# Output projection of a hybrid decoder layer: two blocks of rows by seven products of half depth instead of eight

## The chip, the cores and the metric

The kernel runs on one core of a Trainium2 chip. Its time is the device time of one execution in microseconds (us); three runs are given by their median. The engines are called as the profile calls them: PE (TensorE; PEld its weight loads), DVE (VectorE), ACT (ScalarE), POOL (GpSimd) and SP (SyncE, which issues the DMA transfers).

## The reference

One layer on a sequence of 4096 rows of 1024 columns, in float32. Attention (8 heads, three dilated windows) gives 512 columns, an HGRN2 recurrence (4 heads) the other 512; both are normed per head, gated, and set side by side. The change concerns the last lines:

```python
y_attn = _head_rmsnorm(attn, attn_out_norm_w[layer], ATTN_HEADS) * jax.nn.silu(ag.astype(f32))
y_hgrn = _head_rmsnorm(rec, hgrn_out_norm_w[layer], HGRN_HEADS) * jax.nn.silu(hg.astype(f32))
mixed = jnp.concatenate([y_attn, y_hgrn], axis=-1).astype(x.dtype)
x = x + mixed @ w_out[layer]          # (4096 x 1024) @ (1024 x 1024)
...
return _rmsnorm(x, final_norm_w)
```

## The kernel before

The work stands in three stages: the input projection of attention (the start to about 720 us), then the projections of HGRN interleaved with the attention heads, then the end of attention and the output projection (from about 2370 us).

Every float32 operand is split into a high part and a low part (the rest), and a product is made of three matmuls that add into one PSUM bank: high by high, high by low, low by high. A split is one copy on ACT (the high part) and one subtraction (the low part) on DVE or POOL. The stationary operand of a matmul here is a 128x128 piece of rows transposed, the moving one 128x512 of a weight.

`two` opens four PSUM pools: four banks `att`, two `proj`, one `po`, one `hp1`. A scheduler orders each engine's instructions by its own estimate of when they can run; all DMA transfers are issued by SP, one after the other, in an order that is fixed when the kernel is built. An instruction whose operand is not ready holds up all that stand behind it on its engine.

The mixed rows pass through a tensor in memory, `y_d`. The attention's last step, `finish` (L588 to L630), takes eight blocks of rows of a head: PE transposes (L614, L615) into an `att` bank, DVE multiplies them by weights into the tile `pr` (L617, four times), POOL adds (L620, L621), DVE makes the inverse norm `nrr` in small steps (L625, L626, then L133 to L141), POOL multiplies (L628, L629), and a DMA stores to `y_d` (L630). There is one `pr` tile: the next finish's L617 waits until that store is done.

The output projection goes over 32 blocks of 128 rows. `load_y` reads a block of `y_d` in two halves, transposes them on PE (eight transposes, L885) and splits them (L170, L171). `project` (L183 to L185) makes 24 matmuls of 128x512 for each half of the columns. `residual` adds x on DVE (L915), `final_norm` squares on ACT (L922), scales on DVE (L925) and stores. The weights of the first half of the columns lie in `whi` and `wlo`; those of the second half are split (L873, L874) into `w1hi` and `w1lo`, which take over the tiles `QS` and `KH` once the attention's scores (L434, L435) are done with them; `xr4`, four blocks of x, takes over `KL`.

The input projection already has the form that the change brings to the output projection: `summed_w` builds sums and differences of weight quarters, `load_unit` those of the rows, and `half` (L730 to L736) makes one product of half depth, 12 matmuls.

Of the kernel before, what the change touches and what calls it, by code (L numbers as in the profile page):

```python
# [27 lines left out]
S = 4096  # L28
D = 1024
NB = 32  # L30
KT = 8
# [18 lines left out]
def layer(ctx: ExitStack, tc: tile.TileContext, x, xT, xP, pos, w_in, w_out, nw, anw, hnw, lbraw, fnw,  # L50
          ident_in, mask_in, trih_in, invf_in, out):
    nc = tc.nc
    V, A, G, T = nc.vector, nc.scalar, nc.gpsimd, nc.tensor
    dma = nc.sync.dma_start
# [7 lines left out]
    y_d = dram.tile([S, D], F32, name="y_d")  # L62
# [4 lines left out]
    ident = const.tile([128, 128], F32, name="ident")  # L67
# [5 lines left out]
    wp = mid.enter_context(tc.tile_pool(name="wp", bufs=8))  # L73
    xp = mid.enter_context(tc.tile_pool(name="xp", bufs=2))
# [91 lines left out]
    def split_tile(src, lo_eng, pool, tag, bufs):  # L166

        t = pool.tile([128, 1024], F32R, name=tag, bufs=bufs)
        hi, lo = t[:, 0:512], t[:, 512:1024]
        A.activation(hi, src, AF.Copy)  # L170
        lo_eng.tensor_tensor(lo, src, hi.bitcast(F32), op=ALU.subtract)  # L171
        return t

    def parts(t):
        return t[:, 0:512], t[:, 512:1024]

    def project(X, W):
        ps = ps_t.tile([128, 512], F32, name="att")
        for k in range(KT):
            hi, lo = X[k // 4]  # L180
            c = slice((k % 4) * 128, (k % 4 + 1) * 128)
            whi, wlo = W[k]
            T.matmul(ps, hi[:, c], whi, start=(k == 0), stop=False)  # L183
            T.matmul(ps, hi[:, c], wlo, start=False, stop=False)  # L184
            T.matmul(ps, lo[:, c], whi, start=False, stop=(k == KT - 1))  # L185
        return ps

    def load_pair(t, g):

# [470 lines left out]
    def plain_w(P, j):  # L660

        res = []
        for k in range(4):
            raw = fetch_w(2 * P, 4 * j + k, xp, "raw", 3)
            hi = wp.tile([128, 512], F32R, name="whi", bufs=8)
            lo = wp.tile([128, 512], F32R, name="wlo", bufs=8)
            s = nwt[:, 4 * j + k : 4 * j + k + 1]
            A.activation(hi, raw, AF.Copy, scale=s)
            V.scalar_tensor_tensor(lo, raw, s, hi.bitcast(F32), op0=ALU.mult, op1=ALU.subtract)
            res.append((hi, lo))  # L670
        return res
# [58 lines left out]
    def half(ps, X, W, start=True):  # L730
        for k in range(4):
            c = slice(k * 128, (k + 1) * 128)
            (hi, lo), (whi, wlo) = X, W[k]
            T.matmul(ps, hi[:, c], whi, start=start and k == 0, stop=False, skip_group_check=not start)  # L734
            T.matmul(ps, hi[:, c], wlo, start=False, stop=False, skip_group_check=not start)  # L735
            T.matmul(ps, lo[:, c], whi, start=False, stop=(k == 3), skip_group_check=not start)  # L736

    def plain_products(t, X, W, C0, third=True):

        pa = ps_m.tile([128, 512], F32, name="m")  # L740
        half(pa, X["A11"], W["B11"])
        u2 = p1p.tile([128, 512], F32, name="u2", bufs=2)
        A.activation(u2, pa, AF.Copy)
        pe = None
        if third:
            pe = ps_m.tile([128, 512], F32, name="m")
            half(pe, X["S4"], W["B22"])
        half(pa, X["A12"], W["B21"], start=False)
        A.activation(C0[:, 0], pa, AF.Copy, scale=rstd[:, 2 * t : 2 * t + 1])
        return u2, pe  # L750
# [30 lines left out]
    W = {"B11": plain_w(0, 0)}  # L781
# [5 lines left out]
    X = load_unit(0, tables_done)  # L787
# [3 lines left out]
    for P in range(2):  # L791
        if P:
            W = {"B11": plain_w(1, 0), "B21": plain_w(1, 1)}
# [34 lines left out]
    ps_p = ctx.enter_context(tc.tile_pool(name="ps_p", bufs=2, space=PSUM))  # L828
    ps_t = ctx.enter_context(tc.tile_pool(name="ps_t", bufs=4, space=PSUM))
    ps_o = ctx.enter_context(tc.tile_pool(name="ps_o", bufs=1, space=PSUM))  # L830
    ps_h = ctx.enter_context(tc.tile_pool(name="ps_h", bufs=1, space=PSUM))
    two = ExitStack()
    big = two.enter_context(tc.tile_pool(name="big", bufs=1))
    tp = two.enter_context(tc.tile_pool(name="tp", bufs=2))
    QS = big.tile([128, S], F32R, name="QS")
    KH = big.tile([128, S], F32R, name="KH")
    KL = big.tile([128, S], F32R, name="KL")
    OA = big.tile([128, S], F32, name="OA")
# [5 lines left out]
    att = hp.tile([128, 256], F32, name="att", bufs=1)  # L844
# [4 lines left out]
    X = load_pair(0, 4)  # L849
    W = list(load_w(4))  # L850
    for _ in range(4):
        next(queue[0])
    for g in range(4, 8):
        hvec = load_vec(hp, g - 4)
        for t in range(NB // 2):
            qd, kd, ea = hgrn_gates(t, project_T(X, W))
            hgrn_values(t, project_N(X, W))
            if (g, t) != (7, NB // 2 - 1):
                X = load_pair((t + 1) % (NB // 2), g + (t + 1) // (NB // 2))
# [3 lines left out]
        if g < 7:  # L863
            W = list(load_w(g + 1))


    def fetch_wo(n, k, rp, tag, bufs):
        raw = rp.tile([128, 512], F32, name=tag, bufs=bufs)
        dma(raw, w_out[k * 128 : (k + 1) * 128, n * 512 : (n + 1) * 512])
        return raw  # L870

    def split_wo(raw, hi, lo):
        A.activation(hi, raw, AF.Copy)  # L873
        V.tensor_sub(lo, raw, hi.bitcast(F32))  # L874
        return hi, lo

    def load_y(b):
        res = []
        for hf in range(2):
            yt = xp.tile([128, 512], F32, name="raw", bufs=3)  # L880
            dma(yt, y_d[b * 128 : (b + 1) * 128, hf * 512 : (hf + 1) * 512])
            pt_ = ps_p.tile([128, 512], F32, name="proj")
            for k in range(4):
                c = slice(k * 128, (k + 1) * 128)
                T.transpose(pt_[:, c], yt[:, c], ident)  # L885
            res.append(parts(split_tile(pt_, V, xp, "xs", 5)))
        return res

    WO = [[], []]
    for k in range(KT):  # L890
        raw = fetch_wo(0, k, xp, "raw", 3)
        WO[0].append(split_wo(raw, wp.tile([128, 512], F32R, name="whi", bufs=8), wp.tile([128, 512], F32R, name="wlo", bufs=8)))
    three.close()
    fp = two.enter_context(tc.tile_pool(name="fp", bufs=2))
    raws = [fetch_wo(1, k, fp, "woraw", 4) for k in range(4)]
    fnwt = fp.tile([128, D], F32, name="fnwt", bufs=1)
    dma(fnwt, fnw.partition_broadcast(128))
    take(10 ** 9)
    Y = [load_y(0), load_y(1)]
    ps0 = [project(Y[0], WO[0]), project(Y[1], WO[0])]  # L900
    w1hi = big.tile([128, S], F32R, name="w1hi", tag="QS")
    w1lo = big.tile([128, S], F32R, name="w1lo", tag="KH")
    xr4 = big.tile([128, S], F32, name="xr4", tag="KL")
    for k in range(KT):
        raw = raws[k] if k < 4 else fetch_wo(1, k, fp, "woraw", 4)
        c = slice(k * 512, (k + 1) * 512)
        WO[1].append(split_wo(raw, w1hi[:, c], w1lo[:, c]))
    xrs = {}

    def residual(b, n, ps):  # L910
        if b not in xrs:
            xrs[b] = xr4[:, b % 4 * D : (b % 4 + 1) * D]
            dma(xrs[b], x[b * 128 : (b + 1) * 128, :])
        cn = slice(n * 512, (n + 1) * 512)
        V.tensor_add(xrs[b][:, cn], ps, xrs[b][:, cn])  # L915

    def final_norm(b):
        xr = xrs.pop(b)
        ss = fp.tile([128, 2], F32, name="fss")
        for n in range(2):  # L920
            sq = fp.tile([128, 512], F32, name="fsq")
            A.activation(sq, xr[:, n * 512 : (n + 1) * 512], AF.Square, accum_out=ss[:, n : n + 1])  # L922
        V.tensor_add(ss[:, 0:1], ss[:, 0:1], ss[:, 1:2])
        r = rsqrt(fp, ss[:, 0:1], 1, 1.0 / D, EPS, "fr")
        V.scalar_tensor_tensor(xr, xr, r, fnwt, op0=ALU.mult, op1=ALU.mult)  # L925
        dma(out[b * 128 : (b + 1) * 128, :].rearrange("(u r) c -> r u c", r=16), xr)

    for b in range(2):
        residual(b, 0, ps0[b])
    for b in range(2):  # L930
        residual(b, 1, project(Y[b], WO[1]))
        final_norm(b)
    Yn = load_y(2)
    for b in range(2, NB):
        Yb, Yn = Yn, load_y(b + 1) if b + 1 < NB else None
        for n in range(2):
            residual(b, n, project(Yb, WO[n]))
        final_norm(b)
    two.close()
    mid.close()  # L940

# [47 lines left out]
```

## Time and profile before

| what | value |
|---|---|
| median of three runs | 2758.32 us (2758.07 to 2759.17) |
| the profiled execution | 2760.87 us, its span 2759.1 us |
| mean granted PE clock | 0.966 of full speed |
| busy: PE, DVE, ACT, POOL | 94%, 70%, 61%, 33% of the span |
| memory traffic | 346 MB read, 126 MB written |

The span runs from the first to the last recorded instruction or transfer. A busy share is a mean over stages. In rows of groups the columns are the line, the engine, the operation with output and inputs, their shapes, the count, then busy us and mean ns of one, and after the second bar the idle time of the engine just before them with what ended it. In rows of single instructions: start, duration, engine, line, and in brackets the idle time before it with its releaser. In a table by stretches, each engine's busy us with its count of instructions, then the granted clock, the share of the DMA engines and GB/s.

### The profile page before, as it was taken

The numbers are of one execution on the slowest core, as the hardware profiler recorded it, in microseconds if no ns is written. First come the engines' busy times: TensorE is split into PE (matmuls) and PEld (weight loads), VectorE is DVE, ScalarE is ACT, GpSimd is POOL, SyncE is SP. The second block draws the span as 40 slices with busy tenths as digits, with TensorE's granted clock in tenths as the row PEclk, the third lists the DMA queues.
The fourth block names the chain that finished last, engine by engine and source line by source line (L and its number), as shares of the span: only waits on it lengthen the run. The fifth ranks groups of instructions, "written<-read, shape, count | busy, mean of one in ns | idle before, by whom it ended". The sixth has DMA issues, their size and how long they took to land.

```text
span 2759.1 us, 51828 instructions
## 1 busy us (share of the span) xinstructions
PE 2596.6 (94%) x17330; PEld 2347.1 (85%) x17330; DVE 1936.2 (70%) x5202; ACT 1689.5 (61%) x4719; POOL 919.1 (33%) x900
## 2 busy tenths in 40 slices
PE   6899989999979999899999899999999997899998
PEld 4678867888869989899999899999999996688887
DVE  8777788777637788787787786776777777533443
ACT  8755565555548778678678686687686687222222
POOL 5456636656434464141241231331321421100000
PEclk8999999999979999899999999999999998899999
DMA  6864464444685776774864755746846644444442
GB/s 231 255 181 145 145 200 126 146 144 143 211 235 171 237 232 188 201 187 142 219 178 146 226 162 154 211 143 198 219 137 190 190 141 118 124 137 131 137 132 87
DMA packets 452190, 475.89 MB, mean 172 GB/s; under 512 B 119336, under 2 KB 334420, under 8 KB 451924
## 3 DMA queue, kind: packets, MB, share of 16 engines
q1 hardware_dynamic: 451924, 472.58, 58.0%
q8 instruction: 138, 2.26, 0.4%
q14 instruction: 128, 1.05, 0.1%
HBM read 346.06 MB, written 126.37 MB: 171 GB/s over the span
## 4 chain that ended last, share of the span: by engine, by line
PE 72%; DMA 10%; DVE 8%; ACT 4%; issue 2%; SPq 2%; POOL 2%; DVEq 0%; POOLq 0%; ACTq 0%
PE proj L210 19%; PE po L469 6%; PE m L736 5%; PE m L735 5%; PE m L734 5%; PE att L457 5%; PE att L183 4%; PE att L184 4%; PE att L185 4%; PE att L434 3%; PE att L435 3%; DMA raw<-xP 1%; DMA y_d<-pr 1%; PE proj L885 1%; DMA QS<-qk_d 1%
## 5 line engine op out<-in xcount | busy, mean ns | idle before, releaser
L210 PE MATMUL proj<-xs,whi 128*128 128x256 f32 x2048 | 431.6, 295 | 18.8 <-ACT whi L161 9.3
L210 PE MATMUL proj<-whi,xs 128*128 128x256 f32 x2048 | 432.5, 294 | 4.4 <-DVE hz L317 4.4
L210 PEld LDWEIGHTS proj<-xs,whi 128*128 128x128 f32 x2048 | 333.8, 194 | 25.0 <-ACT whi L161 10.7
L210 PEld LDWEIGHTS proj<-whi,xs 128*128 128x128 f32 x2048 | 335.8, 194 | 6.0 <-DVE hz L317 4.7
L445 DVE CUSTOM_DVE_ANT_0 pt<-att,mask 128x256 f32<-128x256 f32 (+1 forms) x768 | 269.4, 388 | 77.5 <-PE att L435 75.4
L210 PE MATMUL proj<-xs,wlo 128*128 128x256 f32 x1024 | 301.7, 295 | 0.6 <-DVE wlo L162 0.6
L210 PE MATMUL proj<-wlo,xs 128*128 128x256 f32 x1024 | 300.0, 293 | 0.0
L461 DVE TENSOR_TENSOR pl<-att,ph 128x512 fp32r<-128x512 f32 (+1 forms) x384 | 237.4, 625 | 57.5 <-ACT ph L460 53.3
L447 ACT ACTIVATE pt<-pt,ml 128x256 f32<-128x256 f32 (+1 forms) x512 | 238.1, 467 | 57.2 <-DVE ml L445 56.2
L457 PE MATMUL att<-ident,pt 128*128 128x128 f32 x1368 | 229.4, 281 | 5.7 <-ACT pt L447 3.9
L460 ACT ACTIVATE ph<-att 128x512 fp32r<-128x512 f32 (+1 forms) x384 | 203.0, 542 | 47.9 <-PE po L469 29.2
L469 PE MATMUL po<-ph,vh 128*128 128x128 f32 (+1 forms) x856 | 213.7, 279 | 7.2 <-issue 2.7
L469 PE MATMUL po<-pl,vh 128*128 128x128 f32 (+1 forms) x856 | 208.3, 289 | 2.9 <-DVE pl L461 2.9
L210 PEld LDWEIGHTS proj<-xs,wlo 128*128 128x128 f32 x1024 | 198.6, 194 | 2.3 <-issue 1.2
L210 PEld LDWEIGHTS proj<-wlo,xs 128*128 128x128 f32 x1024 | 198.0, 193 | 1.2 <-issue 1.0
L915 DVE TENSOR_TENSOR xr<-att,xr 128x512 f32<-128x512 f32 x64 | 44.3, 692 | 195.7 <-PE att L185 195.7
L469 PEld LDWEIGHTS po<-ph,vh 128*128 128x128 f32 x856 | 167.8, 196 | 12.1 <-issue 6.7
L457 PEld LDWEIGHTS att<-ident,pt 128*128 128x128 f32 x1368 | 163.1, 144 | 11.2 <-ACT pt L447 5.7
L469 PEld LDWEIGHTS po<-pl,vh 128*128 128x128 f32 x856 | 168.3, 197 | 4.2 <-DVE pl L461 3.7
L734 PE MATMUL m<-tw,ss 128*128 128x512 f32 x384 | 155.2, 405 | 15.2 <-ACT tw L170 6.8
L475 ACT ACTIVATE pot<-po 64x512 f32<-64x512 f32 (+1 forms) x256 | 124.2, 485 | 71.0 <-DVE o L579 31.5
L735 PE MATMUL m<-tw,ss 128*128 128x512 f32 x384 | 155.0, 404 | 4.8 <-DVE tw L171 4.8
(256 smaller groups left out, 7591.3 us busy)
## 6 DMA issues: line engine op xcount, KB each, us to landing
xs<-xh_d SPq DMA_DIRECT2D x192, 512.0 KB
xr<-xT SPq DMA_DIRECT2D x128, 256.0 KB
qk_d<-stk SPq DMA_DIRECT2D x128, 256.0 KB
xh_d<-xs SPq DMA_DIRECT2D x64, 512.0 KB
vh<-v_d SPq DMA_DIRECT2D x512, 64.0 KB
raw<-x SPq DMA_DIRECT2D x64, 256.0 KB
v_d<-hl SPq DMA_DIRECT2D x128, 128.0 KB
raw<-xP SPq DMA_DIRECT2D x64, 256.0 KB
```

Of the source, the lines that this page charges most:

```text
L183: T.matmul(ps, hi[:, c], whi, start=(k == 0), stop=False)
L210: m = T.matmul(o, l, r, start=first is None, stop=(k == KT - 1 and g == len(groups) - 1 and n == 2))
L445: V.tensor_tensor_reduce(out=p_, in0=o, in1=mask[:, (1, 4, 16).index(d), 256 - 128 * nk : 256], scale=-0.125, scalar=3e38, op0=ALU.add, op ...
L447: A.activation(p_, p_, AF.Exp, scale=-1.0, bias=m, accum_out=l)
L457: T.transpose(ps[:, n * 128 : (n + 1) * 128], loc[u], ident)
L460: A.activation(ph[:, :w], ps[:, :w], AF.Copy)
L461: V.tensor_sub(pl[:, :w], ps[:, :w], ph[:, :w].bitcast(F32))
L469: T.matmul(po[:, 128 * c : 128 * (c + n)], v, rh, start=(s == 0), stop=(s == len(steps) - 1))
L475: A.activation(t[o : o + 64, c], po[64 - o : 128 - o, c], AF.Copy)
L734: T.matmul(ps, hi[:, c], whi, start=start and k == 0, stop=False, skip_group_check=not start)
L735: T.matmul(ps, hi[:, c], wlo, start=False, stop=False, skip_group_check=not start)
L736: T.matmul(ps, lo[:, c], whi, start=False, stop=(k == 3), skip_group_check=not start)
```

## The change

The output projection takes two blocks of rows at once (16 pairs). With the rows of a pair as A = (A11 A12; A21 A22), blocks by halves of the depth, and the weights as B = (B11 B12; B21 B22), halves of the depth by halves of the columns, it makes seven products of half depth instead of eight. Row sums: S1 = A21 + A22, S2 = S1 - A11, S3 = A11 - A21, S4 = A12 - S2. Weight sums: T1 = B12 - B11, T2 = B22 - T1, T3 = B22 - B12, T4 = B21 - T2. Then u2 = A11·B11 + S2·T2 and u4 = u2 + S1·T1, and the four blocks of the result are A11·B11 + A12·B21; u4 + S4·B22; u2 + S3·T3 + A22·T4; u4 + S3·T3. The diff, cut:

```diff
-    def project(X, W):
...
-    WO = [[], []]
...
-    raws = [fetch_wo(1, k, fp, "woraw", 4) for k in range(4)]
...
+    def load_y(t):
+        a, X = {}, {}
+        for (i, j), (pool, tag, bufs) in (((0, 0), (ps_p, "proj", 2)), ((1, 0), (ps_o, "po", 1)), ((1, 1), (ps_h, "hp1", 1)),
+                                          ((0, 1), (ps_p, "proj", 2))):
+            yt = tp.tile([128, 512], F32, name="vh", bufs=3)
+            dma(yt, y_d[(2 * t + i) * 128 : (2 * t + i + 1) * 128, j * 512 : (j + 1) * 512])
+            a[i, j] = pool.tile([128, 512], F32, name=tag, bufs=bufs)
+            for k in range(4):
+                c = slice(k * 128, (k + 1) * 128)
+                T.transpose(a[i, j][:, c], yt[:, c], ident)
...
+        split("A11", a[0, 0], V)
+        a21 = tp.tile([128, 512], F32, name="o1", bufs=2)
+        A.activation(a21, a[1, 0], AF.Copy)
+        s1 = tp.tile([128, 512], F32, name="pot", bufs=2)
+        V.tensor_tensor(s1, a[1, 1], a21, op=ALU.add)
+        s2 = tp.tile([128, 512], F32, name="pot", bufs=2)
+        V.tensor_tensor(s2, s1, a[0, 0], op=ALU.subtract)
+        split("S2", s2, G, (("pt", 5), ("pt", 5)))
+        split("A12", a[0, 1], V)
+        split("S1", s1, G)
+        V.tensor_tensor(a21, a[0, 0], a21, op=ALU.subtract)
+        split("S3", a21, G, (("pt", 5), ("pt", 5)))
+        V.tensor_tensor(s2, a[0, 1], s2, op=ALU.subtract)
+        split("S4", s2, G, (("qc", 2), ("qc", 2)))
+        split("A22", a[1, 1], V)
...
+    def begin(t, X, third=True):
+        xr = [fp.tile([128, D], F32, name="xr", bufs=4) for _ in range(2)]
+        for i in range(2):
+            dma(xr[i], x[(2 * t + i) * 128 : (2 * t + i + 1) * 128, :])
+        pa = bank()
+        half(pa, X["A11"], WO["B11"])
+        u2 = fp.tile([128, 512], F32, name="u2", bufs=2)
+        A.activation(u2, pa, AF.Copy)
+        if third:
+            third_product(X, xr)
+        half(pa, X["A12"], WO["B21"], start=False)
+        V.tensor_tensor(xr[0][:, c0], pa, xr[0][:, c0], op=ALU.add)
+        return xr, u2
+    def third_product(X, xr):
+        pe = bank()
+        half(pe, X["S4"], WO["B22"])
+        V.tensor_tensor(xr[0][:, c1], pe, xr[0][:, c1], op=ALU.add)
+    def finish_pair(t, X, xr, u2):
+        pb = bank()
+        half(pb, X["S2"], WO["T2"])
+        V.tensor_tensor(u2, pb, u2, op=ALU.add)
+        pc = bank()
+        half(pc, X["S1"], WO["T1"])
+        u4 = fp.tile([128, 512], F32, name="u4", bufs=1)
+        V.tensor_tensor(u4, pc, u2, op=ALU.add)
+        G.tensor_tensor(xr[0][:, c1], u4, xr[0][:, c1], op=ALU.add)
+        final_norm(2 * t, xr[0])
+        G.tensor_tensor(xr[1][:, c1], u4, xr[1][:, c1], op=ALU.add)
+        G.tensor_tensor(xr[1][:, c0], u2, xr[1][:, c0], op=ALU.add)
+        pd = bank()
+        half(pd, X["S3"], WO["T3"])
+        V.tensor_tensor(xr[1][:, c1], pd, xr[1][:, c1], op=ALU.add)
+        half(pd, X["A22"], WO["T4"], start=False)
+        V.tensor_tensor(xr[1][:, c0], pd, xr[1][:, c0], op=ALU.add)
+        final_norm(2 * t + 1, xr[1])
...
+    def summed_wo():
+        bt = {n: big.tile([128, S], F32R, name="w" + n, tag=tag) for n, tag in (("T2", "QS"), ("T1", "KH"), ("T3", "KL"), ("T4", "OA"))}
+        WO.update({n: [None] * 4 for n in ("T1", "T2", "T3", "T4", "B22")})
+        for k in range(4):
+            r = [fp.tile([128, D], F32, name="xr", bufs=4) for _ in range(2)]
+            for j in range(2):
+                dma(r[j], w_out[(4 * j + k) * 128 : (4 * j + k + 1) * 128, :])
+            b11, b12, b21, b22 = r[0][:, c0], r[0][:, c1], r[1][:, c0], r[1][:, c1]
+            def unit(name, src):
+                t = bt[name][:, k * 1024 : (k + 1) * 1024]
+                WO[name][k] = split_wo(src, t[:, c0], t[:, c1])
+            WO["B22"][k] = split_wo(b22, tp.tile([128, 512], F32R, name="ph", bufs=4), tp.tile([128, 512], F32R, name="pl", bufs=4))
+            V.tensor_tensor(b11, b12, b11, op=ALU.subtract)
+            t2 = fp.tile([128, 512], F32, name="u2", bufs=2)
+            V.tensor_tensor(t2, b22, b11, op=ALU.subtract)
+            unit("T2", t2)
+            unit("T1", b11)
+            V.tensor_tensor(b12, b22, b12, op=ALU.subtract)
+            unit("T3", b12)
+            V.tensor_tensor(b21, b21, t2, op=ALU.subtract)
+            unit("T4", b21)
+    X = load_y(0)
+    summed_wo()
+    begun = begin(0, X)
+    for t in range(NB // 2):
+        Xn = load_y(t + 1) if t + 1 < NB // 2 else None
+        if t == 0:
+            early = begin(1, Xn, third=False)
+        finish_pair(t, X, *begun)
...
```

The plain quarters B11 and B21 stay in `whi` and `wlo`. T1 to T4 lie in the attention's tiles `QS`, `KH`, `KL` and `OA`, B22 in its `ph` and `pl`. Up to the end of attention the instructions are the same; 11 lines fewer stand ahead of them, so that L617 is now L606, L630 is L619, and L874 is L859.

Three places show how the instructions now stand. First DVE, at the last-but-two finish: rows of L138 to L141 are the steps of its inverse norm, L579 (now L568) belongs to the last head, L617 (now L606) is the next finish; L982 to L989 are the weights' subtractions for the first two quarters of the depth. Before:

```order
L607 TENSOR_TENSOR den<-den 128x8
L138 TENSOR_TENSOR nrq<-nrr 128x8
L139 TENSOR_TENSOR nrq<-nrq,nrm 128x8
L140 TENSOR_SCALAR nrq<-nrq 128x8
L141 TENSOR_TENSOR nrr<-nrr,nrq 128x8
L579 TENSOR_TENSOR o_29516<-po,pot 64x256 x2
L617 TENSOR_TENSOR pr<-att,wt 128x2x192 x4
```

After, at the same place:

```order
L138 TENSOR_TENSOR nrq<-nrr 128x8
L139 TENSOR_TENSOR nrq<-nrq,nrm 128x8
L568 TENSOR_TENSOR o_29516<-po,pot 64x256
L140 TENSOR_SCALAR nrq<-nrq 128x8
L984 TENSOR_TENSOR u_31992<-xr 128x512
L987 TENSOR_TENSOR xr<-xr 128x512
L141 TENSOR_TENSOR nrr<-nrr,nrq 128x8
L568 TENSOR_TENSOR o_29516<-po,pot 64x256
L989 TENSOR_TENSOR xr<-xr,u_31992 128x512
L982 TENSOR_TENSOR xr<-xr 128x512
L984 TENSOR_TENSOR u_32013<-xr 128x512
```

Subtractions on loaded weights have moved in between the steps of the norm, ahead of L141, whose result POOL's L628 (now L617) waits for.

Second SP, in the same stretch: L630 (now L619) is the store to `y_d`, L542 (now L531) a load of the last head, L881 (now L882) a load of rows from `y_d`, L974 the loads of whole weight rows, L913 (now L923) of x. Before:

```order
L869 DMA woraw<-w_out 128x512 x4
L897 DMA fnwt<-fnw 128x1024
L542 DMA vh<-v_d_67 128x4x128
L630 DMA y_d<-pr 128x8x64
L596 DMA sgt<-sg_d 128x8x64
L881 DMA raw<-y_d 128x512 x5
L542 DMA vh<-v_d_67 128x4x128
L881 DMA raw<-y_d 128x512 x4
```

After:

```order
L619 DMA y_d<-pr 128x8x64
L585 DMA sgt<-sg_d 128x8x64
L974 DMA xr<-w_out 128x1024 x2
L882 DMA vh<-y_d 128x512 x2
L974 DMA xr<-w_out 128x1024 x2
L882 DMA vh<-y_d 128x512 x2
L619 DMA y_d<-pr 128x8x64
```

The loads of the last two quarters of the weights now stand between stores of two finishes, the last of them behind two loads of rows.

Third PE, after the first two products: L724 and L725 are matmuls of `half` with the plain weights, L886 the transposes of rows into the free banks of three pools, and the rows with `ph`, `pl` and `qc` the product S4·B22. Before, the products stood in one piece of 48 behind the last transposes of attention. After:

```order
L724 MATMUL att<-wlo,xs 128x512
L725 MATMUL att<-whi,xs 128x512
L886 MATMUL po<-ident,vh 128x128 x4
L886 MATMUL proj<-ident,vh 128x128 x4
L886 MATMUL hp_32129<-ident,vh 128x128 x4
L886 MATMUL po<-ident,vh 128x128 x4
L886 MATMUL proj<-ident,vh 128x128 x4
L723 MATMUL att<-ph,qc 128x512
L724 MATMUL att<-pl,qc 128x512
L723 MATMUL att<-whi,xs 128x512
```

After the products with plain weights stand 20 transposes, and then the first product that needs the weights' splits and the rows' sums.

More of the change, by code (lines that the diff above doesn't have):

```diff
@@ L175, in parts @@
         return t[:, 0:512], t[:, 512:1024]
-    def project(X, W):
[L178 to L186, printed above, removed]
     def load_pair(t, g):
@@ L864, in layer @@
             W = list(load_w(g + 1))
[L867 to L870, printed above, removed]
     def split_wo(raw, hi, lo):
@@ L875, in split_wo @@
         return hi, lo
[L877 to L887, printed above, removed]
-    WO = [[], []]
-    for k in range(KT):
-        raw = fetch_wo(0, k, xp, "raw", 3)
-        WO[0].append(split_wo(raw, wp.tile([128, 512], F32R, name="whi", bufs=8), wp.tile([128, 512], F32R, name="wlo", bufs=8)))
+    WO = {}
+    for j in range(2):
+        WO[f"B{j + 1}1"] = []
+        for k in range(4 * j, 4 * j + 4):
+            raw = xp.tile([128, 512], F32, name="raw", bufs=3)
+            dma(raw, w_out[k * 128 : (k + 1) * 128, 0:512])
+            WO[f"B{j + 1}1"].append(split_wo(raw, wp.tile([128, 512], F32R, name="whi", bufs=8),
+                                             wp.tile([128, 512], F32R, name="wlo", bufs=8)))
     three.close()
-    fp = two.enter_context(tc.tile_pool(name="fp", bufs=2))
-    raws = [fetch_wo(1, k, fp, "woraw", 4) for k in range(4)]
+    fp = two.enter_context(tc.tile_pool(name="fp", bufs=1))
     fnwt = fp.tile([128, D], F32, name="fnwt", bufs=1)
@@ L898, in layer @@
     take(10 ** 9)
[L899 to L915, printed above, removed]
@@ L917, in final_norm, with split @@
-    def final_norm(b):
-        xr = xrs.pop(b)
-        ss = fp.tile([128, 2], F32, name="fss")
+    def load_y(t):
[8 more added lines that the diff above has]
+                T.transpose(a[i, j][:, c], yt[:, c], ident)
+        def split(name, src, eng, tags=None):
+            if tags is None:
+                X[name] = parts(split_tile(src, eng, xp, "xs", 5))
+                return
+            hi, lo = (tp.tile([128, 512], F32R, name=n, bufs=b) for n, b in tags)
+            A.activation(hi, src, AF.Copy)
+            eng.tensor_tensor(lo, src, hi.bitcast(F32), op=ALU.subtract)
+            X[name] = hi, lo
+        split("A11", a[0, 0], V)
[13 more added lines that the diff above has]
+        split("A22", a[1, 1], V)
+        return X
@@ new lines, in bank @@
+    def bank():
+        return ps_t.tile([128, 512], F32, name="att")
+    c0, c1 = slice(0, 512), slice(512, 1024)
+    def begin(t, X, third=True):
[11 more added lines that the diff above has]
+        return xr, u2
@@ L920, in final_norm @@
+    def final_norm(b, xr):
+        ss = fp.tile([128, 2], F32, name="fss", bufs=2)
         for n in range(2):
-            sq = fp.tile([128, 512], F32, name="fsq")
+            sq = tp.tile([128, 512], F32, name="sgt", bufs=1)
             A.activation(sq, xr[:, n * 512 : (n + 1) * 512], AF.Square, accum_out=ss[:, n : n + 1])
@@ L926, in final_norm @@
         dma(out[b * 128 : (b + 1) * 128, :].rearrange("(u r) c -> r u c", r=16), xr)
[L928 to L938, printed above, removed]
+    def summed_wo():
[3 more added lines that the diff above has]
+            r = [fp.tile([128, D], F32, name="xr", bufs=4) for _ in range(2)]
+            for j in range(2):
+                dma(r[j], w_out[(4 * j + k) * 128 : (4 * j + k + 1) * 128, :])
[21 more added lines that the diff above has]
+        finish_pair(t, X, *begun)
+        if t == 0:
+            third_product(Xn, early[0])
+            begun = early
+        elif Xn:
+            begun = begin(t + 1, Xn)
+        X = Xn
     two.close()
```

## The prediction

> **What bounds the kernel now.** I read the page first, then the end of the kernel by stretches, then single instructions. From the page:
>
> ```profile
> span 2759.1 us, 51828 instructions
> PE 2596.6 (94%) x17330; PEld 2347.1 (85%) x17330; DVE 1936.2 (70%) x5202; ACT 1689.5 (61%) x4719; POOL 919.1 (33%) x900
> PE 72%; DMA 10%; DVE 8%; ACT 4%; issue 2%; SPq 2%; POOL 2%; DVEq 0%; POOLq 0%; ACTq 0%
> ```
>
> TensorE (PE) works 94% of the span and carries 72% of the chain that ends last. Those are means over stages, so the change's own stage has to be read by itself. Two stages bear on it: the output projection, and the input projection, which already runs seven half-depth products. Busy time by stretch:
>
> ```profile
> core 0: us, PE busy (x) PEld busy (x) DVE busy (x) ACT busy (x) POOL busy (x), PEclk, DMA share, GB/s
> 380.00:420.00 40.00, 27.96 (x93) 17.94 (x92) 33.15 (x59) 29.20 (x52) 10.73 (x7) 0.87 0.61 194
> 420.00:460.00 40.00, 35.73 (x153) 28.22 (x153) 35.51 (x56) 20.27 (x39) 27.48 (x21) 0.96 0.45 135
> 500.00:700.00 200.00, 200.00 (x922) 165.54 (x921) 149.80 (x260) 103.03 (x189) 120.10 (x100) 1.00 0.47 142
> 2350.00:2400.00 50.00, 39.05 (x161) 31.65 (x160) 27.24 (x63) 15.80 (x40) 10.73 (x8) 0.76 0.36 104
> 2400.00:2450.00 50.00, 50.00 (x238) 41.75 (x238) 21.20 (x49) 11.42 (x34) 0.00 (x0) 1.00 0.47 146
> ```
>
> From 2400 us on PE is busy in every microsecond at full granted clock (50.00 of 50.00, 1.00), DVE less than half, POOL not at all. Here a matmul saved is time saved. Ahead of it (2350 to 2400) PE is idle 11 us and no engine is full: a chain of single steps, whose last links are these:
>
> ```profile
> 2366.41 1.37 POOL pr L628
> 2367.85 1.60 POOL pr L629
> 2369.47 2.77 DMA y_d<-pr
> 2372.37 0.57 DVE pr L617
> 2372.98 0.80 PE att L183
> ```
>
> The last-but-one finish of attention is scaled on POOL, its tile is stored, DVE may overwrite that tile (L617), and only then the first product starts. Matmuls of the stream:
>
> ```profile
> 2373.57 0.63 PE L184 MATMUL att<-wlo,xs 128*128 128x512 f32 x1
> 2378.69 0.60 PE L184 MATMUL att<-wlo,xs 128*128 128x512 f32 x1
> ...
> 2503.30 1.03 PE L885 MATMUL proj<-ident,raw 128*128 128x128 f32 x8
> 2504.09 0.48 PE L183 MATMUL att<-whi,xs 128*128 128x512 f32 x1
> ...
> 2505.77 0.39 PE L184 MATMUL att<-wlo,xs 128*128 128x512 f32 x1
> 2506.90 0.39 PE L183 MATMUL att<-whi,xs 128*128 128x512 f32 x1
> ...
> 2515.07 1.03 PE L885 MATMUL proj<-ident,raw 128*128 128x128 f32 x8
> ```
>
> Five matmuls take 2506.90 - 2505.77 = 1.13 us, 0.227 each (48 in a block of 2515.07 - 2503.30 = 11.77 us, with 0.79 us for eight transposes, 2504.09 - 2503.30). The first ones after the idle stretch run at 0.427: twelve in 2378.69 - 2373.57 = 5.12 us, 2.4 us lost. The Trainium skill, "TensorE: Matmul & The Clock Gate", section "What's actually happening", has a clock halved after an idle window and restored after a busy one of about 3.4 us. The trace agrees with the halving, but its slow stretch is over 5 us; by the page's figure a restart would cost an estimated 1.7 us instead of 2.4.
>
> **The change part by part.** All is summed against the profiled execution, 2760.87 us (span 2759.1), which is 2.55 above the median 2758.32.
>
> (a) Products. Before: 64 halves of a row block, 24 matmuls each, 1536. After: 16 pairs, seven products of 12 matmuls each, 1344. 192 x 0.2267 (the 11.77 us block less 0.89 for its transposes, by 48) = -43.5 us, all of it in stretches where PE is full. This holds only while PE stays full. A pair of blocks then takes 84 x 0.2267 + 1.78 = 20.8 us instead of 23.5, and must be fed by the others, priced from these rows (2400 to 2740 us, and the two operand-adding lines of the input projection):
>
> ```profile
> L915 DVE TENSOR_TENSOR xr<-att,xr 128x512 f32<-128x512 f32 x58 | 40.1, 692 | 181.3 <-PE att L185 181.3
> L171 DVE TENSOR_TENSOR xs<-proj,xs 128x512 fp32r<-128x512 f32 x56 | 38.7, 692 | 14.4 <-ACT xs L170 10.5
> L925 DVE SCALAR_TENSOR_TENSOR xr<-xr,frr,fnwt 128x1024 f32<-128x1024 f32 x29 | 37.3, 1285 | 1.0
> L922 ACT ACTIVATE fsq<-xr 128x512 f32<-128x512 f32 x58 | 36.6, 631 | 136.5 <-DVE xr L915 136.5
> L170 ACT ACTIVATE xs<-proj 128x512 fp32r<-128x512 f32 x56 | 33.2, 593 | 124.0 <-PE proj L885 124.0
> L139 DVE TENSOR_TENSOR frq<-frq,frm 128x1 f32<-128x1 f32 x29 | 4.6, 160 | 1.0
> L171 POOL TENSOR_TENSOR ss<-xr,ss 128x512 fp32r<-128x512 f32 x12 | 15.4, 1287 | 0.0
> L723 DVE TENSOR_TENSOR xr<-xr 128x512 f32<-128x512 f32 x12 | 21.0, 1752 | 3.6 <-POOL tmp L717 3.6
> ```
>
> Per pair DVE has 13 operations of 0.69, two of 1.29 and ten small ones of 0.16: 13.2 us. ACT has seven splits and two copies of 0.59 and four squares of 0.63, with their small parts about 9.5. POOL has four low parts and three additions of 1.29: 9.0. None comes near 20.8, and the 500 to 700 us stretch shows the same form of product with PE at 200.00 of 200.00 beside a DVE at 75% and a POOL at 60%. So nothing is added for the steady pairs.
>
> (b) Transposes: 28 of them stood ahead of the stream and now about 20 do, so eight more fall into it: 8 x 0.10 = +0.8.
>
> (c) The build of the summed weights. Removed: the split of the second half of the weights, eight DVE operations, 1 MB of early loads and 1 MB later. Added: eight loads of 512 KB, eight subtractions and 20 splits. They stand, by the order, between the steps of the last finishes: ahead of the small step (L141) whose result L628 waits for, hence ahead of the store, hence ahead of the products. Prices:
>
> ```profile
> L874 DVE TENSOR_TENSOR w1lo<-woraw,w1hi 128x512 fp32r<-128x512 f32 x8 | 8.3, 1060 | 0.0
> 2357.64 1.67 DVE L874 TENSOR_TENSOR w1lo<-woraw,w1hi 128x512 fp32r<-128x512 f32 x1
> L617 DVE TENSOR_TENSOR pr<-att,wt 128x384 f32<-128x384 f32 x12 | 6.0, 551 | 7.7 <-DMA y_d<-pr 7.1 <-PE att L615 0.6
> GB/s 181 185 261 294 264 266 150 10 0 0 0 7 186 387 350 395 439 291 305 343 365 335 350 291 287 380 417 402 164 26 0 15 0 0 0 0 0 192 207 186
> ```
>
> 28 operations at the 1.06 us of L874 are 29.7, less the eight removed (8.3): +21.4. DVE's own waits for the stores (7.1 in the groups) hide that much: +14.3 remain. The loads run at about 350 GB/s (last row, 2350 to 2372 us in 40 slices): 2 MB more are 6 us of transfer, but the ring of four tiles of 512 KB lets the third and fourth quarter of the build begin only when the first is used up, and SP, which issues everything in order, has the loads of the last quarter behind loads of y that wait for a PE tile. Most of this runs while DVE works: I take +2. Together +16. The nearest row is the same build in the input projection: between 380 and 460 us PE is idle 12.0 + 4.3 = 16.3 us. Bounds: 0, if all of it falls into time in which DVE waits anyway; above, 28 x 1.67 (the dearest L874) - 8.3 + 6 - 7.1 = 37.
>
> The long L874 overlap POOL's work, and L723 takes 1752 ns in the input projection, where POOL is busy. The Trainium skill, "SBUF — State Buffer", section "Who interferes with whom", says that a DVE instruction with two SBUF inputs contends with a GpSimd instruction that reads SBUF, whichever comes second blocking. The build is made of such instructions, so the page speaks against the change; the trace agrees in 1752 against 692 ns with one input in PSUM.
>
> (d) A second stall: A11·B11 and A12·B21 need plain weights and can run early, but S4·B22 waits for DVE (four additions, the weights' last splits) and for POOL. Bounds 0 and 7 (ten operations of 0.69); taken +3, about four operations, as the others lie behind other transposes. A restart at half clock +2.4; the present one stays.
>
> (e) The first two pairs share tiles with the build (transients): +1, between 0 and one POOL operation twice, 2.6.
>
> (f) The last pair: T4 adds into the bank that DVE must first read (L953), and that waits for POOL. After T1: u4 on DVE 0.69, two additions on POOL 2.58, so 3.27; T3's 12 x 0.227 = 2.72 hide the most of it, then L953 takes 0.69. PE stands 3.27 + 0.69 - 2.72 = 1.2: +1.2, between 0 and 2.5 (a third POOL operation first). Then the end is as now. In the other pairs the next pair's products stand between T3 and T4.
>
> Sum: -43.5 + 0.8 + 16 + 3 + 2.4 + 1 + 1.2 = -19.1. 2760.87 - 19.1 = 2741.8, for the median 2739.2; I say 2740.
>
> **The rivals.**
> - The build is hidden. DVE has idle time in the last finishes, and PE's idle 11 us between 2350 and 2400 may absorb it. Then (c) is 0 to 7: 2722 to 2731 as a median. Against it: the build of the input projection was not hidden, with the same operations.
> - The build is twice as dear. DVE and POOL block each other, loads, splits and stores queue up behind one another: (c) 30 to 37, median 2753 to 2760, the gain nearly or wholly cancelled. For it: L874 up to 1.67 us; against it: POOL does only 11 us of work in 2350 to 2400.
> - Slower, by one mechanism: SP's order in the steady pairs. The fourth y load of a pair stands behind the store of the earlier output block, which waits for the final norm; all later loads stand behind both. If it lands too late, PE stands in every pair. From 16 pairs 15 can stall, so 19/15 = 1.3 us per pair cancel the gain, and 2.2 give +14, 2772. From the pair's start: T2 and T1 5.4, u4 0.7, POOL 1.3, two squares 1.3, the norm's small steps about 2, the scaling 1.3 make 12, with queues on DVE and ACT 13 to 15; then SP goes on. That load lands some 4 us later (the row below, the dearest y load of the chain), at 17 to 19, and is needed at about 20. That is 1 to 3 us of room, the thinnest place of the steady state.
>
> ```profile
> 2342.04 4.00 DMA raw<-y_d
> ```
>
> **How the numbers follow.** Head as counted (2732 to 2750): 0.57. Head hidden: 0.20. Head twice as dear: 0.13, of which 0.04 is still faster, 0.07 within and 0.02 beyond. SP's order: 0.10, of which 0.02 within and 0.08 slower. A measurement of this kernel tells about 0.2%, 5.5 us, from no change: faster below 2752.8, slower above 2763.8. That gives 0.81, 0.09 and 0.10. The range of 8 in 10 reaches from 2720 (head hidden, all other terms small) to 2759 (head twice as dear); beyond it lie SP's order and the worst of the head.
>
> **What would show it.** The products' count 1344, pitch 0.227 and a pair of 20.8 us between transposes with PE full show (a); a pair above 22 shows the third rival, and the group of y loads as PE's releaser names it. The stretch from the last score to the first S4·B22 shows (c) and (d): some 16 + 3 + 2.4 us more than now, with DVE's subtractions between the steps of the norm. The prediction is wrong if the idle time of PE ahead of the stream has not grown, or has grown by more than 30 us, or if DVE's additions of two SBUF tiles reach 1.7 us throughout.

## The result, and the profile after

Seven runs of the changed kernel gave a median of 2742.37 us (2731.08 to 2748.97) against 2759.48 (2758.07 to 2762.99) for the kernel before: 17.1 us less, a ratio of 0.9928 with a 95% interval of 0.9908 to 0.9948. The forecast was 2740, between 2720 and 2759. The profiled execution took 2743.28 us, its span 2741.5.

From the page, then busy time by stretch (columns as before):

```profile
span 2741.5 us, 51929 instructions
PE 2553.6 (93%) x17138; PEld 2308.2 (84%) x17138; DVE 2024.1 (74%) x5310; ACT 1747.1 (64%) x4811; POOL 1069.4 (39%) x1012
PE 69%; DMA 10%; DVE 10%; ACT 4%; issue 3%; POOL 2%; SPq 1%; POOLq 0%; DVEq 0%; ACTq 0%
```

```profile
2320.00:2360.00 40.00, 20.32 (x112) 16.81 (x112) 30.20 (x86) 17.08 (x53) 11.94 (x10) 0.70 0.40 122
2360.00:2400.00 40.00, 21.81 (x88) 17.12 (x88) 32.24 (x62) 19.41 (x42) 8.96 (x8) 0.61 0.54 178
2400.00:2420.00 20.00, 18.36 (x75) 15.37 (x76) 6.74 (x15) 6.25 (x13) 9.46 (x9) 0.84 0.18 52
2420.00:2700.00 280.00, 280.00 (x1345) 233.30 (x1345) 189.52 (x368) 118.19 (x287) 124.25 (x94) 1.00 0.51 151
```

PE has 192 instructions fewer. From 2420 us on it is busy in all of 280 us, with DVE at 68% and POOL at 44%: the pairs run as forecast. Ahead of that, PE stands for 38 of 80 us (2320 to 2400), with DVE at 78%. The group of the last addition of a pair gives the length of one, (2717.4 - 2428.6) / 14 = 20.63 us, against two blocks of 11.77 before:

```profile
L955 DVE TENSOR_TENSOR xr<-att,xr x15: 678/691/692, 2428.6 to 2717.4; 128x512 f32<-128x512 f32 x15
```

The last finishes and the first products, single instructions of DVE (the first row is of the kernel before), then of PE:

```profile
2366.10 0.16 DVE L141 TENSOR_TENSOR nrr<-nrr,nrq 128x8 f32<-128x8 f32 x1
2329.11 0.69 DVE L982 TENSOR_TENSOR xr<-xr 128x512 f32<-128x512 f32 x1 [1.93 <-DMA xr<-w_out]
2331.73 0.16 DVE L141 TENSOR_TENSOR nrr<-nrr,nrq 128x8 f32<-128x8 f32 x1
2377.54 0.17 DVE L141 TENSOR_TENSOR nrr<-nrr,nrq 128x8 f32<-128x8 f32 x1
2386.30 1.01 DVE L606 TENSOR_TENSOR pr<-att,wt 128x384 f32<-128x384 f32 x2
```

```profile
2386.90 0.79 PE L723 MATMUL att<-whi,xs 128*128 128x512 f32 x1 [3.44 <-DVE pr L606]
2401.64 1.09 PE L886 MATMUL po<-ident,vh 128*128 128x128 f32 x4 [4.25 <-DMA vh<-y_d]
2403.23 0.78 PE L723 MATMUL att<-ph,qc 128*128 128x512 f32 x1
2728.47 0.50 PE L723 MATMUL att<-wT,xs 128*128 128x512 f32 x1 [1.58 <-DVE xr L953]
```

The last step of the last-but-one norm starts at 2377.54 (before: 2366.10), the first product at 2386.90 (2372.98). PE then stands 4.25 us for a load of rows, S4·B22 starts at 2403.23, and in the last pair PE stands 1.58 us.

**A mark for comparing.** The changed kernel's own runs lie 18 us apart, more than most differences below. The time of the last HGRN step on DVE shows where much of that comes from; it is the last start in these rows of the kernel before, the changed kernel, and the changed kernel again (`same`):

```profile
L397 DVE SCALAR_TENSOR_TENSOR hgv<-hgv,hrr x128: 332/347/1450, 789.1 to 2318.0; 128x128 f32<-128x128 f32 x128
L386 DVE SCALAR_TENSOR_TENSOR hgv<-hgv,hrr x128: 332/347/1450, 789.7 to 2319.2; 128x128 f32<-128x128 f32 x128
L386 DVE SCALAR_TENSOR_TENSOR hgv<-hgv,hrr x128: 332/347/1448, 795.3 to 2327.7; 128x128 f32<-128x128 f32 x128
```

Between two executions of the same kernel the mark moved 8.5 us, in code that the change leaves alone; from the mark to the end of the span it is 422.3 and 421.1 us (2741.5 - 2319.2, 2748.8 - 2327.7). The kernel before has 441.1. So the change is worth 18.8 to 20.0 us from the mark on, and the kernels below (each is described with its experiment) are compared by that length first, with the ratio to the kernel before beside it. The columns give the time from the mark to the first matmul of the stream, to the first of S4·B22, and to the end of the span:

| kernel | mark to first product | mark to S4·B22 | mark to end | ratio to before, 95% interval |
|---|---|---|---|---|
| before | 55.0 | | 441.1 | 1 |
| changed (first profile; `same`) | 67.7; 67.8 | 84.0; 83.2 | 422.3; 421.1 | 0.9928 (0.9908 to 0.9948); 0.9944 (0.9928 to 0.9959) |
| no_build | 52.2 | 60.8 | 398.2 | 0.9847 (0.9829 to 0.9865) |
| no_lo | 59.4 | 67.8 | 406.1 | 0.9885 (0.9868 to 0.9902) |
| no_reload | 70.8 | 77.3 | 417.7 | 0.9917 (0.9899 to 0.9935) |
| early | 71.3 | 81.6 | 418.4 | 0.9914 (0.9897 to 0.9930) |
| norm_first | 56.6 | 80.1 | 419.4 | 0.9905 (0.9886 to 0.9924) |
| nf_early | 62.8 | 81.4 | 419.9 | 0.9914 (0.9896 to 0.9931) |
| y6 | 74.0 | 83.1 | 420.0 | 0.9926 (0.9911 to 0.9941) |
| pool | 69.4 | 78.3 | 416.0 | 0.9921 (0.9905 to 0.9936) |
| sums_pool | 71.9 | 88.4 | 425.8 | 0.9934 (0.9919 to 0.9949) |
| sums_pool2 | 66.2 | 79.9 | 421.2 | 0.9913 (0.9899 to 0.9926) |
| sums_pool4 | 59.5 | 69.6 | 412.9 | 0.9887 (0.9859 to 0.9914) |

Lengths come from one profile each, and `same` shows about a microsecond between two; differences below some 3 us are not leaned on. From S4·B22 to the end the changed kernel takes 338.3 and 337.9 us and no_build 337.4: what the build costs is lost ahead of S4·B22.

### The profile page after: what moved, and what is told of

Read it like the earlier page. It is cut to its first block, busy times and chain, and to the rows that moved or that the text cites. A ratio compares the mean times of both kernels' runs of the same rounds, so it can differ in the third digit from the quotient of the medians.

```text
span 2741.5 us, 51929 instructions
## 1 busy us (share of the span) xinstructions
PE 2553.6 (93%) x17138; PEld 2308.2 (84%) x17138; DVE 2024.1 (74%) x5310; ACT 1747.1 (64%) x4811; POOL 1069.4 (39%) x1012
## 4 chain that ended last, share of the span: by engine, by line
PE 69%; DMA 10%; DVE 10%; ACT 4%; issue 3%; POOL 2%; SPq 1%; POOLq 0%; DVEq 0%; ACTq 0%
PE proj L199 19%; PE po L458 6%; PE m L725 6%; PE m L723 6%; PE m L724 6%; PE att L446 4%; PE att L723 3%; PE att L724 3%; PE att L725 3%; PE att L423 3%; PE att L424 3%; DMA y_d<-pr 1%; DMA raw<-x 1%; DVE pr L606 1%; DMA raw<-w_in 1%
## 5 line engine op out<-in xcount | busy, mean ns | idle before, releaser
L449 ACT ACTIVATE ph<-att 128x512 fp32r<-128x512 f32 (+1 forms) x384 | 203.4, 542 | 47.4 <-PE po L458 28.6
L723 PE MATMUL m<-tw,ss 128*128 128x512 f32 x384 | 154.9, 404 | 15.2 <-ACT tw L170 7.4
L724 PE MATMUL m<-tw,ss 128*128 128x512 f32 x384 | 154.5, 402 | 4.1 <-DVE tw L171 4.1
L725 PE MATMUL m<-tw,ss 128*128 128x512 f32 x384 | 155.7, 406 | 0.0
```

Of the source, the lines that this page charges most:

```text
L449: A.activation(ph[:, :w], ps[:, :w], AF.Copy)
```

## The experiments

**same, no_build: what the build costs.** The second is the changed kernel with

```diff
     def summed_wo():
-        (loads, subtractions, splits)
+        WO.update({"T1": stale(KH), "T2": stale(QS), "T3": stale(KL), "T4": stale(QS), "B22": WO["B11"]})
```

> The changed kernel once more, unaltered, for a second profile and as the mark for the others of this call. All theories: about 2742 us, and pairs of 20.8 us from the third on. Its runs lay between 2731 and 2749, those of the kernel before between 2758 and 2763: if that spread is made ahead of the stream (waits for the weights' loads and the stores), the two profiles of this kernel differ before 2410 us and not behind it.

> Leaves out the build of the summed weights: no loads, subtractions or splits; the products T1 to T4 take what the attention left in its tiles, and S4 is multiplied by B11 in place of B22. By the prediction's term (c) and by the first product's later start (2386.90 against 2372.98, less 1.3 that had come up before) the build costs 13 to 16 us: 2726 to 2730 expected. If the transposes and the rows' loads delay the stream and not the build: less than 5 us saved, 2737 or more.

`same` gave 2743.94, and the two profiles differ ahead of the stream as said, but not by the loads: the mark above lies ahead of all of them. Without the build the median was 2718.7, less than either theory expected. PE fills up from the first product on (the span, the mark, two stretches):

```profile
span 2718.8 us, 51849 instructions
L386 DVE SCALAR_TENSOR_TENSOR hgv<-hgv,hrr x128: 331/347/1449, 788.5 to 2320.6; 128x128 f32<-128x128 f32 x128
2318.00:2373.00 55.00, 31.72 (x183) 27.33 (x184) 34.43 (x110) 24.50 (x73) 15.49 (x13) 0.75 0.46 133
2373.00:2400.00 27.00, 27.00 (x122) 22.34 (x123) 14.85 (x30) 9.88 (x22) 17.88 (x15) 0.95 0.17 51
```

From the mark it saves 24.1 and 22.9 us against the two profiles. Against the kernel before it is 42.9 us shorter. Of these, 2.8 lie ahead of the first product (52.2 for 55.0); that the split which the change removes no longer stands there may be the reason, but no run shows it. The other 40.1 are the stretch from the first product to the end, 386.1 us before and 346.0 in no_build: what the seven products save.

**no_reload, early: is it the loads?** The chain of the changed kernel puts three loads of weights, 14.6 us, on the way to the end:

```profile
2323.30 5.79 DMA xr<-w_out
2363.26 4.56 DMA xr<-w_out
2374.47 4.20 DMA xr<-w_out
```

```diff
 no_reload:
-            r = [fp.tile([128, D], F32, name="xr", bufs=4) for _ in range(2)]
+            if k < 2: (load as before, held.append(r))
+            r = held[k % 2]
 early: (ahead of take(10 ** 9))
+    for k in range(4):
+        wr.append([xp.tile([128, D], F32R, name="xs", bufs=5).bitcast(F32) if k < 2 else fp.tile([128, D], F32, name="xr", bufs=4) for _ in range(2)])
+        for j in range(2):
+            dma(wr[k][j], w_out[(4 * j + k) * 128 : (4 * j + k + 1) * 128, :])
```

> The third and fourth quarter of the build are made from the loaded tiles of the first two, with no loads of their own: half the bytes, the same 28 operations on DVE (the sums are then of wrong quarters). Theory 'loads': the chain of the changed kernel has 5.79 + 4.56 + 4.20 us of weight loads, the last two fall away: 2733. Theory 'operations' (the prediction's: 14 of 16 us are DVE's work in front of the norm): at most 2 us saved, 2740 or more.

> All eight weight loads have tiles of their own (four more in the tiles of the split rows), so none waits for the build to free one; the operations are the same 28, in the scheduler's own order. Theory 'loads': the waits of 5.79, 4.56 and 4.20 us on the chain go, 10 to 14 us saved, 2730 to 2734. Theory 'order': less than 4 us saved beyond what a changed order gives, 2740 or more.

From the mark they saved 4.6 and 3.9 us against the first profile, 3.4 and 2.7 against the second; their medians, 2739.6 and 2740.44, lie some 6 us above what theory "loads" expected. Taking the loads away gave most of their time to the next thing in line: in both the first product came later than in the changed kernel. In no_reload the scheduler put 32 of the build's operations on DVE ahead of the last step of the last-but-one norm, in the changed kernel 26. Theory "loads" falls as the main cause.

**norm_first, nf_early: is it the order?** DVE may start the build only behind the norms (`norms` holds the last step of each finish's norm; `after` sets an order and no wait):

```diff
+            first = norms[-3] if k < 2 else norms[-2]
+            after(V.tensor_tensor(b11, b12, b11, op=ALU.subtract), first)     # and the three others
+            WO[name][k] = split_wo(src, t[:, c0], t[:, c1], norms[-2])        # low part after norms[-2]
```

> The same instructions, but DVE may do the build's subtractions of the first two quarters only behind the norm of the last finish but two, and the rest of the build only behind that of the last but one. Without the build the changed kernel took 25 us less, with half the loads 4 less. Theory 'order' (DVE's operations in front of the norm hold up the store and with it the stream): the last-but-one norm ends some 15 us earlier, 10 to 20 us saved, 2724 to 2734. Theory 'loads': the third and fourth quarter wait for their loads all the same and only move the stall behind the first products: less than 5 us saved. Theory 'amount' (28 operations have to run somewhere before T2 is needed): the same, less than 5.

> Both: own tiles for all weight loads, and the build behind the norms. 'Order' and 'loads' together: up to the 25 us that the kernel without the build saved, less what of DVE's 17 us of build work stands between the last scores and the first T2: 2720 to 2728. If 'order' alone matters: as norm_first, within 3.

The order did what it was made for: the first product came 11.1 us sooner (56.6 for 67.7). The end came 2.9 us sooner, 1.7 against the second profile. The rest was given back ahead of S4·B22, where PE now waits and DVE has hardly a gap (norm_first, by stretch, and the longest new wait):

```profile
2377.00:2400.00 23.00, 13.35 (x47) 9.57 (x48) 21.70 (x32) 11.60 (x21) 6.96 (x5) 0.72 0.53 195
2395.94 1.11 PE L892 MATMUL proj<-ident,vh 128*128 128x128 f32 x4 [5.39 <-DVE o L913]
```

DVE is busy 21.70 of 23 us, and PE waits for a row sum (L913) that stands behind the build. nf_early, with both edits, was no better, where 2720 to 2728 had been expected. By the mark theory "amount" is what is left. The runs are less clear: the interval of norm_first's ratio ends at 0.9924, below where that of `same` begins (0.9928), though it overlaps that of the changed kernel's first runs. So the order on DVE may be worth more than 3 us; nf_early's 0.9914 does not confirm it.

**no_lo: is it the amount?** The 20 low parts on DVE are left out:

```diff
-                WO[name][k] = split_wo(src, t[:, c0], t[:, c1])
+                A.activation(t[:, c0], src, AF.Copy)
+                WO[name][k] = t[:, c0], t[:, c0]
```

> Leaves out the 20 low parts of the summed weights and of B22 on DVE (the high part stands in for the low one); loads, the eight... sixteen subtractions in all and ACT's 20 high parts stay, in the scheduler's own order. In norm_first DVE was full from 2377 to 2400 us and the rows' sums stood behind the build: if DVE's amount of work is the bound, 20 x 0.6 = 12 us or more of the build's 24 go, counted from the last HGRN step: 407 to 411 instead of 421 to 422.5. If ACT's high parts or the loads are the bound: 418 or more.

no_lo reached 406.1 us from the mark: 16.2 less than the first profile (15.0 than the second), where 407 to 411 was expected of theory "amount". The interval of its ratio lies below both of the changed kernel. Its span, mark and first matmul of S4·B22:

```profile
span 2735.3 us, 51905 instructions
L386 DVE SCALAR_TENSOR_TENSOR hgv<-hgv,hrr x128: 333/347/1455, 788.4 to 2329.2; 128x128 f32<-128x128 f32 x128
2396.95 0.48 PE L723 MATMUL att<-ph,qc 128*128 128x512 f32 x1
```

What it leaves out is, in the changed kernel, 14.9 us of DVE's work (the first three rows):

```profile
L859 DVE TENSOR_TENSOR wT<-xr,wT 128x512 fp32r<-128x512 f32 x12 | 9.6, 815 | 0.0
L859 DVE TENSOR_TENSOR wT<-u,wT 128x512 fp32r<-128x512 f32 x4 | 2.7, 678 | 0.0
L859 DVE TENSOR_TENSOR pl<-xr,ph 128x512 fp32r<-128x512 f32 x4 | 2.6, 678 | 0.0
L982 DVE TENSOR_TENSOR xr<-xr 128x512 f32<-128x512 f32 x4 | 3.8, 956 | 2.9 <-DMA xr<-w_out 2.9
L987 DVE TENSOR_TENSOR xr<-xr 128x512 f32<-128x512 f32 x4 | 3.8, 950 | 0.0
L989 DVE TENSOR_TENSOR xr<-xr,u 128x512 f32<-128x512 f32 x4 | 3.3, 822 | 0.0
L984 DVE TENSOR_TENSOR u<-xr 128x512 f32<-128x512 f32 x4 | 2.8, 706 | 1.9 <-DMA xr<-w_out 1.8
```

These are all of the build's groups on DVE in the changed kernel (2320 to 2400 us): 36 operations, 28.6 us. Two thirds of the build's price goes with its low parts, with loads, subtractions and ACT's part still there. Shown is thus that DVE's amount of work ahead of S4·B22 is the larger part of the price.

That it comes out nearly one to one is in part chance. The first product of the changed kernel runs at half the granted clock, that of no_lo at the full one (stretches of the two; the clock is the third number from the end):

```profile
2386.90:2392.10 5.20, 5.20 (x12) 4.01 (x13) 1.43 (x3) 0.00 (x0) 0.00 (x0) 0.50 0.88 334
2388.60:2391.30 2.70, 2.70 (x14) 2.13 (x12) 2.67 (x6) 1.29 (x3) 1.19 (x1) 1.00 0.96 379
```

Its twelve matmuls take 0.427 us each in the one and 0.228 in the other, so an estimated 2.4 of the 16.2 us are the clock's: twelve times the difference.

**y6, pool.** Rows' loads into six tiles instead of three; and 16 of the low parts on POOL:

```diff
 y6:
-            yt = tp.tile([128, 512], F32, name="vh", bufs=3)
+            yt = tp.tile([128, 512], F32, name="vh", bufs=3) if j == 0 else xp.tile([128, 512], F32, name="raw", bufs=3)
 pool:
+                G.tensor_tensor(t[:, c1], src, t[:, c0].bitcast(F32), op=ALU.subtract)
```

> The y loads of the right half of the depth go into the three free tiles that the plain weights were read into, so six tiles instead of three hold rows ahead. In the changed kernel PE waits 4.25 us for a y load after the first two products, and about 2.4 us more go to the half clock behind it. If the three tiles are what delays that load: 4 to 7 us saved, 2735 to 2738. If the load waits for the stores to y_d or stands behind others on SP: less than 2 us saved. In the steady pairs nothing is expected of either.

> The low parts of T1 to T4 (16 of the 20 splits) go from DVE to POOL, at 1.29 us each there by the rows before. DVE is 16 x 0.68 = 11 us lighter ahead of the stream. Theory 'DVE's work in front': 5 to 10 us saved, 2734 to 2739. Rival: POOL's two steps of the last-but-one finish queue behind up to 16 x 1.29 = 21 us of splits and hold up the same store: slower than the changed kernel by up to 10, 2745 to 2753.

y6 saved 2.3 or 1.1 us from the mark, no more than `same` can tell. The wait of 4.25 us for rows is gone in it (9.1 us from the first product to S4·B22 for the changed kernel's 16.3), but the first product came 6.3 us later, behind this wait for DVE:

```profile
2391.77 0.69 PE L604 MATMUL att<-ident,o 128*128 128x128 f32 x2 [9.67 <-DVE o L568]
```

Whether the six tiles or the later start took the wait for rows away stays open. In pool both theories had a part: 6.3 or 5.1 us saved from the mark (its ratio, 0.9921, shows little of it), less than the 12.3 us by which DVE's work is lighter. One of POOL's splits stood between the two steps of the last-but-one finish (1.27 us between L617 and L618), and splits beside DVE's work stretched to 1.72; the rest of the difference was not taken apart.

**sums_pool, sums_pool2, sums_pool4: a better version.** All subtractions go to POOL, from weights loaded early as in `early`, and DVE's low parts stand behind the last-but-one norm; then more orders in turn (`s4s[0]` is the subtraction that makes the first pair's S4; `exps` and `gates` hold ACT's last step of each norm and POOL's last step of each finish). In sums_pool4 the subtractions are also called behind `take(10 ** 9)`, which writes the rest of attention:

```diff
 sums_pool:  (in weight_sums, called ahead of take(10 ** 9))
+            G.tensor_tensor(b11, b12, b11, op=ALU.subtract)      # and the three others
 sums_pool2:
+                WO[name][k] = split_wo(src[k], t[:, c0], t[:, c1], norms[-2] if name == "T2" else s4s[0])
 sums_pool4:
+            if k > 1:
+                after(x, gates[-3])                              # POOL: behind its last step of that finish
+            after(h, exps[-2] if j is not s4s[0] else his[2])    # ACT's high parts: behind the norm, or behind S4's
```

> All 16 subtractions go to POOL, from weights loaded into tiles of their own as soon as these are free, ahead of the last finishes; DVE keeps the 20 low parts, behind the last-but-one norm. If DVE's amount is the bound: some 10 us less of it ahead of S4·B22; counted from the last HGRN step 408 to 414 (changed kernel 422), median 2728 to 2735. If POOL's steps of the finishes queue behind the subtractions: 420 or more.

> As sums_pool, and of the low parts only those of B22 and T2 stand ahead of the first pair's row sums; those of T1, T3 and T4 stand behind. The first pair's S4·B22 needs only B22: it starts as early as in the kernel without the build plus 5 us, and 13.6 us of products (five of 2.72) cover most of the other 12 low parts (7 to 8 us). 402 to 408 counted from the last HGRN step, 2722 to 2730. If the order of the first products makes PE wait for T1 all the same: as sums_pool.

> As sums_pool2, with two orders more: POOL makes the sums of the third and fourth quarter only behind its last step of the finish ahead (in sums_pool2 four of them stood in front of that step, 4.9 us), and ACT makes high parts only behind its last step of the last-but-one norm (they stood in front of the last softmax, 5.4 us), those of T1, T3 and T4 only behind S4's. If the build's cost is its place on three engines: both delays go, 10 us less than sums_pool2, 408 to 413 from the last HGRN step (changed kernel 421 to 422.5), median 2727 to 2734. If DVE's amount alone decides (20 low parts, 15 us, between the last scores and T4): 417 or more.

sums_pool took 425.8 us from the mark, as its second theory had it, and sums_pool2 421.2 instead of 402 to 408. POOL's queue shows one reason (sums_pool2):

```profile
2342.99 1.04 POOL L621 TENSOR_TENSOR pr<-pr,nrr 128x512 f32<-128x512 f32 x1 [1.03 <-DVE nrr L143]
2343.99 1.26 POOL L893 TENSOR_TENSOR raw<-xr 128x512 f32<-128x512 f32 x1
2345.21 1.26 POOL L894 TENSOR_TENSOR xr<-xr 128x512 f32<-128x512 f32 x1
2346.43 1.26 POOL L893 TENSOR_TENSOR raw<-xr 128x512 f32<-128x512 f32 x1
2347.65 1.26 POOL L894 TENSOR_TENSOR xr<-xr 128x512 f32<-128x512 f32 x1
2348.87 1.26 POOL L622 TENSOR_TENSOR pr<-pr,sgt 128x512 f32<-128x512 f32 x1
```

Four sums of weights stand between the two steps that lead to the store, 4.9 us. With that and ACT's queue put in order, sums_pool4 reached 412.9 us from the mark, 8 to 9 less than the changed kernel, and 2732.65 against 2761.11, a ratio of 0.9887 (0.9859 to 0.9914). It beats the kernel before, and the changed kernel by the mark; their ratios' intervals, from separate comparisons, overlap between 0.9908 and 0.9914. DVE has the same work in sums_pool2 and sums_pool4, so the 8.3 us between them are a matter of order on POOL and ACT: DVE's amount alone does not decide.

sums_pool4 still has 14.7 us more than no_build: 7.3 ahead of the first product, 1.5 from there to S4·B22, 5.9 behind it. PE's waits for loads of rows, 7.0 us in sum, explain little of it, since no_build has 5.4 (3.65 and 1.75); the rest was not taken apart.

## Why the prediction was right, point by point

The forecast was 2740 and the median 2742.37. The products came out as reasoned; the size of the build came out by luck.

- (a), the products: right. a + b + f forecast -41.5; from the first product to the end no_build is 40.1 us shorter than the kernel before. (b) was not measured by itself. A pair takes 20.63 for the forecast 20.8.
- (c), the build: the sum nearly held, its working did not. Forecast +16 ahead of the first product; measured 67.7 - 55.0 = 12.7. The step that failed is the count times the price: "28 operations at the 1.06 us". The loop makes four subtractions for each of four quarters, 16 and not 8, so there are 36 operations; they took 28.6 / 36 = 0.79 us and not 1.06. That the two errors cancel, 28.6 for 29.7, is luck.
- (c), the mechanism: DVE's work as the larger part is confirmed by no_lo. That its place in front of the norm is what costs is not: norm_first moved it, and by the mark the loss came back ahead of S4·B22. The loads, taken at +2, cost 3 to 5 by no_reload and early, near the limit of what the lengths tell.
- (d), the second stall: forecast 3 + 2.4 with DVE and POOL as its releasers. From the first product to S4·B22 the changed kernel takes 16.3 and 15.4 us, no_build 8.6: 7.7 and 6.8 more. The releaser was another one, a load of rows (4.25 us); behind it the clock is at half once more (0.84 in the mean from 2400 to 2420 us), as forecast.
- (e): forecast +1; behind S4·B22 the changed kernel takes 0.9 and 0.5 us more than no_build, which is within what two profiles of one kernel differ by.
- (c) to (e) together: forecast 22.4 against the kernel before. The build costs 24.1 and 22.9 by no_build, but 2.8 of that no_build is ahead of the kernel before by its earlier first product: 21.3 and 20.1.
- (f): 1.58 us for the forecast 1.2, by the wait that was named.
- The rivals: "hidden" would be no_build's 398; the build was not hidden. "Twice as dear" did not come either: (c) is 12.7, not 30 to 37. SP's order in the steady pairs: PE waits for nothing from 2420 to 2700. How much room the fourth load has was not tried.
- The port rule of the Trainium skill, "SBUF — State Buffer", section "Who interferes with whom", shows in single instructions. Two operations of one line of DVE, the second beside POOL's L618:

```profile
2368.99 0.68 DVE L987 TENSOR_TENSOR xr<-xr 128x512 f32<-128x512 f32 x1
2378.97 1.59 POOL L618 TENSOR_TENSOR pr<-pr,sgt 128x512 f32<-128x512 f32 x1
2379.36 1.75 DVE L987 TENSOR_TENSOR xr<-xr 128x512 f32<-128x512 f32 x1
```

  0.68 us alone, 1.75 beside it, as the rule has it. POOL's L618 took longer too, 1.59 for the 1.27 of the finish before. But POOL is busy for only 20.9 of the 80 us (2320 to 2400), so the mean stayed at 0.79: a contention rule gives the price of one instruction, and the other engine's share of the time gives how often it is paid.

## What to carry to other kernels

A saving in matmuls is kept where the engine is full, and what has to be built for it is paid where the engine waits; here 40 us were won and 20 to 21 paid. The first can be counted beforehand; for the second, count every instruction of the loop and ask what it stands in front of on each engine. When a chain shows waits for loads, take the loads away before believing it: of 14.6 us of them some 3 to 5 were won. Compare variants from a mark inside the profile where the common part ahead of it moves by more than the difference sought, and from more than one profile of each where the difference is a few microseconds.

## What the runs showed of the hardware that was not expected

In two profiles of the changed kernel the last HGRN step starts at 2319.2 and 2327.7 us, 8.5 us apart, with the same instructions ahead of it; the stretch behind it differs by 1.2 us. Over eight profiles in which that part of the kernel was left alone (before, changed, same, no_build, no_lo, no_reload, norm_first, pool) the step starts between 2318.0 and 2329.2 us. What moves in the first 2300 us stays open.

After PE has stood, how long the clock stays at half differs between kernels: the first matmuls of the stream run at about 0.43 us each for 6.1 us in the kernel before (2372.98 to 2379.12) and for 2.7 us in norm_first (2377.09 to 2379.79), and in no_lo the first product runs at full clock from its start.
